# Turned values leave PSUM in one copy, and a piece of the sample's convolution is started during the prompt's output projection

## The chip, the cores and the metric

The kernel runs on one core of a Trainium2 chip. The metric is device time in microseconds (us) of one execution. The kernel before took 1496.22 us (median of three runs, 1496.03 to 1497.55); its profiled execution took 1495.0 us.

## The reference, cut to what matters

One layer of a bidirectional encoder trunk with shared weights is applied to two inputs: a prompt of 512 tokens and a sample of 1024 tokens, both 1024 wide, in float32.

```python
h = rmsnorm(x); z = h @ w_in                 # columns: q 512, k 128, v 128, ca 512, cb 512
a_out = window_attn(q, k, v, bias, band, sink)   # |q-k| <= 128, 8 heads, 2 key/value heads of 64
c = ca * sigmoid(cb)
c = dwconv(c, conv_dw_w, conv_dw_b)          # 31 taps along the sequence, 512 channels
c = silu(layernorm(c))
x = x + concat([a_out, c]) @ w_out
u = dwconv(rmsnorm(x) @ w_up, ffn_dw_w, ffn_dw_b)  # 3 taps, 2 x 2816 channels
x = x + (silu(u[:, :2816]) * u[:, 2816:]) @ w_down
y = rmsnorm(x)
```

## The kernel before

Every matrix product is made of three float32r products: each operand is split into a rounded high part (a ScalarE cast or activation) and a low part (operand minus high part, on VectorE or GpSimd), and TensorE adds hi x hi, hi x lo and lo x hi in one PSUM bank. Lines L315 to L317 are these three products of the input and up projections, L796 to L798 those of the output projection. Activations lie with channels on the 128 partitions and 512 tokens along the row.

PSUM has eight banks, each one tile of 128x512 float32: a (three), u (two), b (two) and c (one). Each kind of work may take certain letters. SBUF is cut into slots (h: 61 of 2 KB, q: 15 of 4 KB, and some others); a tile keeps its slot until its last reader has run. In the rows of a profile `h<-b` means that an h slot is written from a b bank.

The stages, with their rough times in the profile:

- **Input projection, 0 to 278 us.** `step` runs one chunk of 128 output columns for 512 tokens (24 matmuls), and `evac` takes the bank apart: convolution inputs go through a gate (L424 folds the sample's), keys and queries are split and stored, values are turned. For the values (`kind "v"`) the scaled tile is turned by four TensorE transposes (L456) into a fresh bank. Then for each of the two key/value heads, ScalarE casts its half of the columns (L463, 128x256), VectorE subtracts that from the bank to get the low part (L464), and for the sample the result is sent to DRAM (L466). This happens three times: once for the prompt, at 88 us, and twice for the sample, at 153 and 166 us. All four operations read the bank, and the sample's copies come back in `load_kv` after the projection. Beside the sample's chunks, `prompt_attention` runs as side work: scores L650, softmax L654, L663, turned scores L692 (cast L694, subtract L695), and the products with the values L706 and L707.
- **Prompt's output projection, 278 to 326 us.** The generator `prompt_out` loads the weights of w_out (L821 in pairs, L817 alone), splits them (`split_wo`: cast L828, subtract L829), runs `out_half` for four blocks of 128 tokens and two halves of the columns, and then `make_h2`, the second RMSNorm (scale L854) with its turn into eight tiles (`transposed`: L274, L276, L277; banks u, b and c). The loop `while out` counts its steps in n; past n = 18 every fourth step also starts one unit of the sample's attention.
- **Prompt's FFN, first half, 337 to 629 us,** with the rest of the sample's attention and its convolution ("late" work) beside it.
- **Sample's output projection, 630 to 720 us, then the sample's FFN and both down projections to the end.** TensorE's order from 720 us on is the same in both kernels.

The convolution runs in `taps`: a bank c accumulates most taps on VectorE (first tap L366, the others L352), a few taps per accumulator are made on ScalarE (L340, L343) and summed on GpSimd (L344), and L360 adds the two sums and frees the bank. `tick`, called with the matmul groups, raises `pace["credit"]`, and work is drawn from `mid` (the accumulator that is open), `convs` (the prompt's channels) or `late` (the sample's) while the credit is positive; a step costs 0.13 + 512/960 = 0.66 of it. The sample's first late set works on sums of neighbouring columns (`csum`) and has ten taps on VectorE.

The order of instructions on each engine comes from a scheduler that simulates the program written here and places what it finds ready first; the written order, the slots and the banks are its input. From then on each engine works strictly in its order.

## Time and profile before

| | us |
|---|---|
| median of three runs | 1496.22 |
| profiled execution, own time | 1495.0 |
| its span from first to last instruction | 1493.2 |
| TensorE busy | 1473.5 |
| VectorE busy | 1118.7 |
| ScalarE busy | 803.4 |
| GpSimd busy | 776.1 |

PE stands for TensorE, PEld for its weight loads, DVE for VectorE, ACT for ScalarE, POOL for GpSimd, SP for the engine whose queue issues most DMAs. A timeline row reads: start, duration, engine, line and operation, output from inputs, count, and in brackets the idle time of the engine before it with what ended that. Matmuls are pipelined, so one shows about 0.39 us though the next starts 0.23 us after it. A group row gives the count, the busy time and mean ns of one, and the idle time before its instructions.

### The profile page before, as it was taken

The page shows a single profiled execution, that of the slowest core. Times are in us where ns is not written, and L with a number is a line of the kernel's source. Part 1 is how long each engine was busy: PE and PEld are TensorE (multiplying, and loading weights), DVE is VectorE, ACT ScalarE, POOL GpSimd, SP SyncE. Part 2 cuts the span into 40 slices and gives each one's busy share as a digit, 9 for nine tenths or more (in the row PEclk, how much of TensorE's full clock was granted, in tenths as well). Part 3 has the DMA queues.
Part 4 walks back from the last instruction along what each step waited for, and adds up shares of the span by engine and source line. Part 5 has one row for each costly group of instructions (what it writes and reads, how often), then busy time and mean ns, then how long its engine had stood idle before and what let it go on. Part 6 is the DMA issues. An engine that isn't in the chain of part 4 may idle for free.

```text
span 1493.2 us, 19866 instructions
## 1 busy us (share of the span) xinstructions
PE 1473.5 (99%) x6736; PEld 1211.8 (81%) x6736; DVE 1118.7 (75%) x1512; ACT 803.4 (54%) x1421; POOL 776.1 (52%) x687
## 2 busy tenths in 40 slices
PE   9999999999999999999999999999999999999998
PEld 7788787878888888788788788888888888888886
DVE  6877945648988887675768888888887856577874
ACT  7524455567778776653465444454444543343355
POOL 3554353338779766332436565665555251135546
PEclk9999999999999999999999999999999999999999
DMA  9555331844444454663214333333332495356644
GB/s 369 193 153 146 95 104 35 240 162 140 123 141 135 131 179 142 215 208 106 71 57 141 134 128 126 128 124 123 129 133 79 144 330 173 117 194 216 221 166 162
DMA packets 124625, 228.19 MB, mean 153 GB/s; under 512 B 20419, under 2 KB 45763, under 8 KB 124396
## 3 DMA queue, kind: packets, MB, share of 16 engines
q1 hardware_dynamic: 124092, 226.37, 46.4%
q8 instruction: 53, 0.87, 0.2%
q10 hardware_dynamic: 432, 0.56, 0.1%
q14 instruction: 48, 0.39, 0.1%
HBM read 166.83 MB, written 61.10 MB: 153 GB/s over the span
## 4 chain that ended last, share of the span: by engine, by line
PE 87%; DVE 4%; DMA 3%; POOL 3%; ACT 2%; issue 2%; SPq 0%; POOLq 0%; DVEq 0%; ACTq 0%
PE w L1194 8%; PE w L1195 8%; PE w L1196 8%; PE w L1527 7%; PE w L1526 7%; PE w L1528 7%; PE b L315 4%; PE b L317 4%; PE b L316 4%; PE u L315 4%; PE u L317 4%; PE u L316 4%; PE a L650 1%; PE a L692 1%; PE u L797 1%
## 5 line engine op out<-in xcount | busy, mean ns | idle before, releaser
L163 POOL TENSOR_TENSOR q<-q,q 128x1024 fp32r<-128x1024 f32 x66 | 159.3, 2414 | 68.1 <-ACT q L162 43.4
L1074 POOL TENSOR_TENSOR q<-q,q 128x512 fp32r<-128x512 f32 x81 | 116.0, 1441 | 127.3 <-ACT q L1180 127.3
L1074 DVE TENSOR_TENSOR h<-h,h 128x512 fp32r<-128x512 f32 (+1 forms) x152 | 129.5, 881 | 57.8 <-ACT h L1082 23.1
L1528 PE MATMUL w<-h,h 128*128 128x512 f32 x432 | 168.1, 389 | 0.0
L1526 PE MATMUL w<-h,h 128*128 128x512 f32 x432 | 168.1, 389 | 0.0
L1527 PE MATMUL w<-h,h 128*128 128x512 f32 x412 | 160.3, 389 | 0.0
L1194 PE MATMUL w<-h,q 128*128 128x512 f32 x368 | 143.8, 391 | 1.1 <-ACT w L1285 0.7
L1196 PE MATMUL w<-h,q 128*128 128x512 f32 x368 | 143.7, 390 | 0.0
L1195 PE MATMUL w<-h,q 128*128 128x512 f32 x347 | 135.5, 390 | 0.0
L1082 ACT CAST h<-h 128x512 fp32r<-128x512 f32 x116 | 69.2, 620 | 105.4 <-DVE h L1074 30.8
L1074 POOL TENSOR_TENSOR h<-h,h 128x512 fp32r<-128x512 f32 (+1 forms) x38 | 52.2, 1375 | 141.7 <-ACT h L1509 110.4
L315 PE MATMUL b<-h,q 128*128 128x512 f32 x312 | 123.2, 395 | 1.9 <-DVE h L464 1.3
L317 PE MATMUL b<-h,q 128*128 128x512 f32 x312 | 122.4, 393 | 0.0
L316 PE MATMUL b<-h,q 128*128 128x512 f32 x312 | 122.1, 391 | 0.0
L315 PE MATMUL u<-h,q 128*128 128x512 f32 x272 | 106.8, 393 | 0.0
L316 PE MATMUL u<-h,q 128*128 128x512 f32 x272 | 106.8, 393 | 0.0
L317 PE MATMUL u<-h,q 128*128 128x512 f32 x272 | 106.7, 392 | 0.0
L162 ACT CAST q<-q 128x1024 fp32r<-128x1024 f32 x66 | 69.1, 1048 | 55.4 <-PE u L316 16.3
L352 DVE SCALAR_TENSOR_TENSOR c<-d,cvw,c 128x512 f32<-128x512 f32 x128 | 96.0, 750 | 1.6
L344 POOL TENSOR_TENSOR h<-h,h 128x512 f32<-128x512 f32 x62 | 81.7, 1318 | 27.1 <-ACT h L343 22.5
L1526 PEld LDWEIGHTS w<-h,h 128*128 128x128 f32 x432 | 81.1, 188 | 17.0
L1528 PEld LDWEIGHTS w<-h,h 128*128 128x128 f32 x432 | 81.1, 188 | 16.8
(476 smaller groups left out, 4002.5 us busy)
## 6 DMA issues: line engine op xcount, KB each, us to landing
q<-in_laid_w_up SPq DMA_DIRECT2D x88, 512.0 KB, 3.7
ga<-q SPq DMA_DIRECT2D x65, 256.0 KB, 2.2
h<-gap SPq DMA_DIRECT2D x57, 256.0 KB, 3.5
h<-ga SPq DMA_DIRECT2D x57, 256.0 KB, 3.5
h<-in_w_down SPq DMA_DIRECT2D x52, 256.0 KB, 3.4
q<-in_laid_w_in SPq DMA_DIRECT2D x22, 512.0 KB, 4.3
gap<-h SPq DMA_DIRECT2D x44, 256.0 KB, 3.1
q<-in_x_sample SPq DMA_DIRECT2D x15, 512.0 KB, 6.9
```

The lines of the kernel that those rows point to most:

```text
L163: (nc.vector if dve else nc.gpsimd).tensor_tensor(lo[:], raw[:], hi[:].bitcast(F32), op=ALU.subtract)
L315: nc.tensor.matmul(out, whi[:, kc, :], hi[:], start=(kc == 0), stop=False)
L316: nc.tensor.matmul(out, whi[:, kc, :], lo[:], start=False, stop=False)
L317: nc.tensor.matmul(out, wlo[:, kc, :], hi[:], start=False, stop=(kc == KC - 1))
L352: nc.vector.scalar_tensor_tensor(acc[:], src(t), w(t), acc[:], op0=ALU.mult, op1=ALU.add)
L1074: (eng or nc.vector).tensor_tensor(out, a, b, op=ALU.subtract)
L1194: nc.tensor.matmul(out, whi[:, s], hi[:], start=(start and c == 0), stop=False, **go)
L1195: nc.tensor.matmul(out, whi[:, s], lo[:], start=False, stop=False, **go)
L1196: nc.tensor.matmul(out, wlo[:, s], hi[:], start=False, stop=(stop and c == 3), **go)
L1526: nc.tensor.matmul(out, sh[:, c], th[:], start=(p == 0 and not seeded), stop=False, **go)
L1527: nc.tensor.matmul(out, sh[:, c], tl[:], start=False, stop=False, **go)
L1528: nc.tensor.matmul(out, sl[:, c], th[:], start=False, stop=(p == NPAIR - 1), **go)
```

## The change

Two edits. In the evacuation of the values, one ScalarE copy takes the whole turned bank into an SBUF tile; the casts read that tile, and the low parts are made on GpSimd instead of VectorE, also from that tile. The stores to DRAM follow both heads. In the loop around `prompt_out`, the steps n = 19 to 26 raise the credit by 0.3 each, once the prompt's channels are done, and draw late work from it: about four steps of the sample's first late accumulator. Lines behind the first edit are one higher in the profile after, lines behind the second five.

```diff
+OL = (18, 0.3, 26)
...
-            vs = []
-            for kv in range(NKV):
-                v = sb.tile([4, P], F32R)
-                head = slice(kv * HD, (kv + 1) * HD)
-                rest = slice((1 - kv) * HD, (2 - kv) * HD)
-                nc.scalar.copy(v[:, :, head], src[:, :, head])
-                nc.vector.tensor_tensor(v[:, :, rest], src[:, :, head], v[:, :, head].bitcast(F32), op=ALU.subtract)
-                if g == 1:
-                    nc.sync.dma_start(vsd[:, n, kv], v[:].bitcast(F32))
-                vs.append(v)
+            vs = [sb.tile([4, P], F32R) for _ in range(NKV)]
+            heads = [slice(kv * HD, (kv + 1) * HD) for kv in range(NKV)]
+            whole = sb.tile([4, P])
+            nc.scalar.copy(whole[:], src)
+            for v, head, rest in zip(vs, heads, heads[::-1]):
+                nc.scalar.copy(v[:, :, head], whole[:, :, head])
+                nc.gpsimd.tensor_tensor(v[:, :, rest], whole[:, :, head], v[:, :, head].bitcast(F32), op=ALU.subtract)
+            if g == 1:
+                for kv in range(NKV):
+                    nc.sync.dma_start(vsd[:, n, kv], vs[kv][:].bitcast(F32))
...
         advance(out)
         n += 1
+        if OL[0] < n <= OL[2] and (mid or not convs):
+            pace["credit"] += OL[1]
+            while late and pace["credit"] > 0:
+                pace["credit"] -= advance(mid[0] if mid else late)
```

Since the scheduler orders the whole program, the edits move instructions elsewhere too. Three places follow. In the rows the first number of a name is its slot or bank, the second the tile.

ScalarE at the sample's first values, before; `b0_49` is the bank with the turned values:

```order
L663 ACTIVATE h32_248_1523,s11_247_1519<-h32_248_1523,s10_246_1518 128x385
L463 CAST h44_243_1507<-b0_49_1502 128x4x64
L663 ACTIVATE h31_249_1529,s11_247_1519<-h31_249_1529,s10_246_1518 128x385
L663 ACTIVATE h15_250_1543,s11_247_1519<-h15_250_1543,s10_246_1518 128x385
L463 CAST h19_244_1511<-b0_49_1502 128x4x64
```

and after:

```order
L664 ACTIVATE h31_250_1527,s11_249_1523<-h31_250_1527,s10_248_1522 128x385
L462 COPY h16_246_1511<-b0_49_1504 128x512
L664 ACTIVATE h15_251_1533,s11_249_1523<-h15_251_1533,s10_248_1522 128x385
L464 CAST h44_244_1509<-h16_246_1511 128x4x64
L464 CAST h19_245_1510<-h16_246_1511 128x4x64
```

The copy L462 is the bank's only reader; both casts stand together behind the second softmax activation and read SBUF.

TensorE at the start of the prompt's output projection, before; `a1_122` is the last product of the prompt's scores and values, `u1_126` the first output bank:

```order
L706 MATMUL a1_122_2665<-h38_418_2646,h18_160_923 128x512
L315 MATMUL b0_123_2685<-h42_98_437,q8_400_2519 128x512
L316 MATMUL b0_123_2685<-h43_99_438,q8_400_2519 128x512
L317 MATMUL b0_123_2685<-h42_98_437,q10_401_2520 128x512
L707 MATMUL a1_122_2665<-q13_419_2647,h18_160_923 128x512
L706 MATMUL a1_122_2665<-q4_420_2661,h18_160_923 128x512
L707 MATMUL a1_122_2665<-q9_421_2662,h18_160_923 128x512
L796 MATMUL u1_126_2815<-h56_449_2783,h23_229_1421 128x512
```

and after:

```order
L771 MATMUL a2_118_2621<-ident_82,h38_415_2598 128x128 x4
L756 MATMUL u0_124_2714<-ident_82,h2_83_354 128x128
L756 MATMUL u0_124_2714<-ident_82,h27_141_744 128x128
L756 MATMUL u0_124_2714<-ident_82,h17_198_1177 128x128
L756 MATMUL u0_124_2714<-ident_82,h26_291_1808 128x128
L707 MATMUL a1_122_2671<-h38_421_2652,h18_160_921 128x512
L708 MATMUL a1_122_2671<-q13_422_2653,h18_160_921 128x512
L707 MATMUL a1_122_2671<-q4_423_2667,h18_160_921 128x512
L708 MATMUL a1_122_2671<-q9_424_2668,h18_160_921 128x512
L797 MATMUL u1_126_2821<-h56_452_2789,h23_230_1423 128x512
```

The projection's matmuls (L316 to L318, earlier L315 to L317) are all done ahead of this piece, the turn `a2_118` moved from among them (28 rows up) to here, and the four products and eight turns stand in a row. Slot h38 holds `h38_415`, which that turn reads, and then `h38_421`, the cast for the first product.

VectorE at the same place, after; `q13_422` is the subtract for the second product, L830 the weights' low parts:

```order
L417 TENSOR_TENSOR b0_123_2691<-b0_123_2691,d1_125_569 128x512
L761 BN_STATS s31_430_2719<-u0_124_2714 128x6
L830 TENSOR_TENSOR h42_465_2814<-h58_450_2785,h43_464_2813 128x512
L425 SCALAR_TENSOR_TENSOR c3_425_2686<-h29_416_2618,b0_123_2691 128x256x2
L762 BN_AGGR s32_431_2720<-s31_430_2719 128x2
L696 TENSOR_TENSOR q13_422_2653<-a0_120_2647,h38_421_2652 128x512
L830 TENSOR_TENSOR h55_453_2790<-q2_419_2636,h56_452_2789 128x512
L765 TENSOR_SCALAR h15_433_2726<-u0_124_2714,s32_431_2720,s0_432_2721 128x512
L830 TENSOR_TENSOR h53_455_2794<-q2_419_2636,h54_454_2793 128x512
L830 TENSOR_TENSOR h18_492_2986<-h9_480_2962,h21_491_2985 128x512
L830 TENSOR_TENSOR h58_496_3011<-h8_481_2964,h59_495_3010 128x512
```

Before, this engine's order had the splits of the first two weight pairs (`q2`, `q0`) ahead of the last evacuation; now they follow it, and the third chunk's low part comes nine operations behind `q13_422`.

TensorE at the end of the prompt's FFN, before; `u0_339` is the last up projection, `a2_332` the last scores:

```order
L317 MATMUL u0_339_6375<-h17_546_3298,q13_1028_6316 128x512
L650 MATMUL a0_333_6296<-q10_439_2763,h47_993_6070 128x256
L650 MATMUL a0_333_6296<-q8_440_2764,h47_993_6070 128x256
L796 MATMUL c0_346_6544<-h0_1051_6459,h51_1048_6453 128x512
L797 MATMUL c0_346_6544<-h56_1052_6460,h51_1048_6453 128x512
L798 MATMUL c0_346_6544<-h0_1051_6459,h10_1049_6454 128x512
L796 MATMUL c0_346_6544<-h46_1054_6465,h51_1048_6453 128x512
L692 MATMUL a1_336_6340<-ident_82,h49_996_6077 128x128
L692 MATMUL a1_336_6340<-ident_82,h52_997_6083 128x128
L692 MATMUL a1_336_6340<-ident_82,h30_998_6101 128x128
L692 MATMUL a1_336_6340<-ident_82,h32_999_6107 128x128
L650 MATMUL a2_332_6290<-q10_439_2763,h47_993_6070 128x256
```

and after:

```order
L693 MATMUL a1_336_6346<-ident_82,h13_999_6083 128x128
L693 MATMUL a1_336_6346<-ident_82,h12_1000_6089 128x128
L651 MATMUL a2_332_6296<-q10_442_2769,h16_996_6076 128x256
L651 MATMUL a2_332_6296<-q8_443_2770,h16_996_6076 128x256
L693 MATMUL a1_336_6346<-ident_82,h45_1001_6107 128x128
L693 MATMUL a1_336_6346<-ident_82,h1_1002_6113 128x128
L316 MATMUL u0_335_6331<-h32_545_3283,q11_1021_6253 128x512
L317 MATMUL u0_335_6331<-h14_546_3284,q11_1021_6253 128x512
```

The scores `a2_332` came after the last up projection; now they come among the matmuls of the last but one, 45 rows ahead of the last.

Two more moves have no rows here. On VectorE the ten `csum` taps of the late set, which stood behind the prompt's turn, now stand among the evacuations of the input projection, in rows 208 to 222 of its order, with only their ScalarE and GpSimd offloads left beside the output projection. Their bank c is not free again until after `make_h2`, whose turn therefore goes round the two b and two u banks.

## The prediction

> **What bounds the kernel now.** The first view is the head of the page: the span and the engines' shares.

> ```profile
> span 1493.2 us, 19866 instructions
> PE 1473.5 (99%) x6736; PEld 1211.8 (81%) x6736; DVE 1118.7 (75%) x1512; ACT 803.4 (54%) x1421; POOL 776.1 (52%) x687
> ```

> PE works in 1473.5 of 1493.2 us, so the change can take away only idle PE time, at most 19.7 us, and can add to it. PE's matmuls stay, so the time is a sum over places where PE waits. The second view, PE's list of waits, names them; the columns are total us, times, longest.

> ```profile
> PE a L706 <- ACT h L694: 1.8, 1, 1.8
> PE b L315 <- DVE h L464: 1.3, 1, 1.3
> PE c L274 <- DVE q L854: 0.5, 1, 0.5
> ```

> The third view gives each engine's load in stretches of 40 us where the change acts: after the length, busy us (and instructions) of PE, its weight loads, DVE, ACT and POOL, then PE's clock and the DMA's share.

> ```profile
> 120.00:160.00 40.00, 37.41 (x182) 30.84 (x181) 37.40 (x74) 19.81 (x46) 16.11 (x22) 1.00 0.43 132
> 200.00:240.00 40.00, 39.86 (x196) 33.27 (x195) 15.75 (x35) 19.50 (x40) 17.40 (x19) 1.00 0.36 99
> 280.00:320.00 40.00, 39.88 (x187) 32.74 (x186) 20.23 (x41) 16.63 (x39) 11.98 (x18) 1.00 0.79 234
> 600.00:640.00 40.00, 37.91 (x179) 30.48 (x178) 26.66 (x51) 26.64 (x54) 15.97 (x12) 0.96 0.76 255
> ```

> The two middle ones have next to no PE idle time to remove (39.86 and 39.88 of 40). The first lost 2.6 us at full clock, the last 2.1 us, and its clock is 0.96. The new order touches five places; I name them A to E in order of time and price each.

> **A, the sample's first turned values (152 to 157 us).** The timeline shows the chain on the bank.

> ```profile
> 153.62 0.35 ACT L463 CAST h<-b 128x256 fp32r<-128x256 f32 x1
> 154.52 0.62 PE L650 MATMUL a<-h,h 128*128 128x384 f32 x2 [1.08 <-DVE s L654]
> 156.03 0.37 ACT L463 CAST h<-b 128x256 fp32r<-128x256 f32 x1 [0.76 <-DVE h L464]
> 156.63 0.41 DVE L464 TENSOR_TENSOR h<-b,h 128x256 fp32r<-128x256 f32 x1
> 157.18 0.47 PE L315 MATMUL b<-h,q 128*128 128x512 f32 x1 [1.34 <-DVE h L464]
> ```

> Bank b is held from 153.62 until 157.04 because the second subtract stands behind other DVE work. PE idles 1.08 + 1.34 = 2.4 us there. After the change one ScalarE copy frees the bank. No 128x512 COPY is in this trace; the nearest rows are a 64x512 copy and a 128x512 cast.

> ```profile
> L714 ACT COPY h<-a 64x512 f32<-64x512 f32 x21 | 12.2, 582 | 12.7 <-PE a L707 12.5
> L694 ACT CAST h<-a 128x512 fp32r<-128x512 f32 x54 | 31.1, 577 | 12.1 <-PE a L692 8.3 <-DMA qsd<-h 3.2 <-DVE q L695 0.5
> ```

> I take 0.58. In the new order the copy stands behind one exponential, so it runs 153.6 to 154.2. PE takes the projection next, idle from 153.4 to about 154.2, 0.8 us: **A = -1.6** (bounds -2.4 to 0). The casts and the two GpSimd subtracts are hidden: the sample's values are read back only after the input projection. The nearest row for a subtract on POOL is twice as wide (1.32 us), so one costs between 0.66 and 1.32 and six cost 4 to 8 us of a POOL that is half idle; DVE loses 6 x 0.41 = 2.5 us. Were a ScalarE copy no faster than two casts and a wait, A would be 0.

> ```profile
> L344 POOL TENSOR_TENSOR h<-h,h 128x512 f32<-128x512 f32 x62 | 81.7, 1318 | 27.1 <-ACT h L343 22.5 <-DVE h L961 1.8 <-ACT h L340 1.8
> ```

> **B, 247 to 250 us.** Here PE waits for the low part of turned scores.

> ```profile
> 247.97 0.50 PE L707 MATMUL u<-q,h 128*128 128x512 f32 x1 [0.81 <-DVE q L695]
> ```

> The new order puts one L424 (1.10 us, next fence) ahead of that subtract; part of it falls into a wait that is there already: **B = +0.6** (0 to +1.1).

> **C, the start of the prompt's output projection.** The change's words put the convolution's taps beside this projection. The order doesn't: all ten of the channel's DVE taps go ahead into the input projection, to about 220 to 231 us, where DVE has 15.75 of 40 us busy. By the rows of L366 (place D) and L352, 0.81 + 9 x 0.75 = 7.6 us; they cost nothing there, and without that slack they would delay the projection's evacuations by up to as much.

> ```profile
> L352 DVE SCALAR_TENSOR_TENSOR c<-c,csum,c 128x512 f32<-128x512 f32 x36 | 27.0, 750 | 0.5
> L343 ACT ACTIVATE h<-c,csum 128x512 f32<-128x512 f32 x20 | 14.0, 720 | 1.7 <-DMA cvd<-h 1.6 <-PE u L798 0.2
> ```

> What does cost is that the loads of the first two weight pairs are issued later on SP, their splits move behind other DVE work, and the turned scores' last products move with them. Before, that start was nearly smooth:

> ```profile
> 282.57 0.39 PE L796 MATMUL u<-h,h 128*128 128x512 f32 x1
> 283.08 0.50 PE L797 MATMUL u<-h,h 128*128 128x512 f32 x1
> 283.42 0.40 PE L798 MATMUL u<-h,h 128*128 128x512 f32 x1
> 283.65 0.40 PE L796 MATMUL u<-h,h 128*128 128x512 f32 x1
> ```

> Matmuls follow each other at 0.23 us (283.42, 283.65); the step from 282.57 to 283.08 lost 0.28. Now the rows for the new order, from the timeline and from the groups of 230 to 330 us:

> ```profile
> 269.86 1.28 DVE L829 TENSOR_TENSOR h<-q,h 128x512 fp32r<-128x512 f32 x2
> ...
> 284.35 0.60 PE L770 MATMUL a<-ident,h 128*128 128x128 f32 x4
> 284.70 0.48 PE L796 MATMUL u<-h,h 128*128 128x512 f32 x1
> ```

> ```profile
> L829 DVE TENSOR_TENSOR h<-h,h 128x512 fp32r<-128x512 f32 x12 | 9.2, 782 | 4.7 <-ACT h L828 4.5
> L416 DVE TENSOR_TENSOR b<-b,d 128x512 f32<-128x512 f32 x2 | 1.4, 696 | 0.2 <-PE b L317 0.2
> L424 DVE SCALAR_TENSOR_TENSOR c<-q,b 128x512 f32<-128x512 f32 x2 | 2.2, 1102 | 0.0
> L760 DVE BATCH_NORM_STATS2 s<-u 128x6 f32<-128x512 f32 x2 | 1.4, 698 | 2.6 <-PE u L755 2.6
> L695 DVE TENSOR_TENSOR q<-a,h 128x512 fp32r<-128x512 f32 x3 | 2.0, 678 | 0.2 <-ACT h L694 0.2
> L776 ACT ACTIVATE q<-a,vecs 128x128 f32<-128x128 f32 x4 | 1.5, 456 | 0.5 <-PE a L770 0.5
> ```

> Call 0 the end of the input projection's last matmul. PE then turns eight tiles (0.35 for four, 284.35 to 284.70; so 0.7) and wants the first product of scores and values. Its operand is a ScalarE cast (0.58) that now stands behind four L776 (1.5), which need the first four turns: ready at about 0.4 + 1.5 + 0.6 = 2.5, a wait of 1.8. The second product needs the subtract that in DVE's order comes after an evacuation (0.70), a BN_STATS (0.70), a split (0.78) and an L424 (1.10): with its own 0.68 ready at 4.0, against PE at 2.7, a wait of 1.3. Eighteen matmuls and four turns later (4.0 + 4.5 = 8.5) PE needs the low part of the third weight chunk, nine DVE operations behind that subtract, most of them splits of 0.64 (two in 1.28) to 0.78. At 0.71 each it is ready at 4.0 + 6.4 = 10.4: a wait of 1.9. Sum 5.0, less the 0.28: **C = +4.7**. Bounds: +2, if the splits' order is harmless and only the first wait stays; +7, if the cast is also late behind splits that wait for their DMA.

> The clock belongs here too. At the end of the prompt's FFN the trace shows what idle time did to it.

> ```profile
> 628.92 0.48 PE L650 MATMUL a<-q,h 128*128 128x256 f32 x2
> 631.22 0.50 PE L706 MATMUL a<-h,h 128*128 128x512 f32 x1 [1.81 <-ACT h L694]
> 632.32 0.67 PE L797 MATMUL c<-h,h 128*128 128x512 f32 x1
> 632.79 0.63 PE L798 MATMUL c<-h,h 128*128 128x512 f32 x1
> ```

> After one wait of 1.81 us the step went from 0.23 to 0.47 us, and the stretch's mean clock fell to 0.96: 0.04 x 40 = 1.6 us lost. The waits at A, 2.4 us in two pieces, cost no clock (1.00 in 120 to 160 us). C has 1.8 + 1.3 us of waits close together, so I count one such drop: **clock at C = +1.6** (0 to +3.2).

> [...]

> **D, the prompt's second RMSNorm and turn (326 to 341 us).**

> ```profile
> 339.43 0.75 DVE L277 SCALAR_TENSOR_TENSOR h<-c,vecs,h 128x512 fp32r<-128x512 f32 x1 [0.40 <-ACT h L276]
> 340.69 0.81 DVE L366 TENSOR_SCALAR c<-c,csum,vecs 128x512 f32<-128x512 f32 x1
> ```

> The late convolution takes bank c at 340.69, after the turn has used it. With the new order the accumulator holds c through the turn, which has four banks instead of five. On POOL one more offloaded sum (L344, 1.32) stands ahead of the root (L146, L147) that releases L854, for which PE waits 0.5 already, and on ScalarE one more offload (L343, 0.72) ahead of the evacuations that free a bank for the first up projection. **D = +2.0** (1.3 + 0.7; bounds 0 to +3).

> **E, the end of the prompt's FFN (629 to 641 us).** The last scores were issued after the last up matmul (628.92), so nothing covered their softmax. The new order issues them 45 PE rows earlier, some 9 us of matmuls. The 1.81 us and the clock's 1.6 go, some 0.2 stays: **E = -3.2** (-3.6 to 0). The FFN between D and E keeps its work on PE, and DVE is lighter by the 7.6 us.

> **Sum:** -1.6 + 0.6 + 4.7 + 1.6 + 2.0 - 3.2 = +4.1. The profiled execution took 1495.0 us (its span and 1.8 around it), so 1499.1; the median, 1496.22, lies 1.2 above that execution, so 1500.3. I predict **1500**.

> **The rivals.** *Faster, 1492.* A and E hold, and the start of the output projection stays as smooth as it was: DVE is busy only 20.23 of 40 us there and catches up. Then 1496.2 - 1.6 - 3.2 + 0.6 = 1492. For it: the two gains remove waits that the list names, with a simple mechanism. Against it: the order of DVE is fixed, and idle time elsewhere in the stretch can't be used.
> *No measurable change, 1496.* C costs 2 without a clock drop, D 2: -1.6 + 0.6 + 2 + 2.0 - 3.2 = -0.2. For it: the terms have both signs. The change then does little of what it says, since the taps moved to a place where DVE idled.
> *The clock holds at C, 1498.7.* All else as in my sum: 4.1 - 1.6 = +2.5. The trace shows 2.4 us of split waits at A that left the clock alone.
> *Slower still, 1504.* ScalarE's cast at C waits behind a split whose weight lands late: C = +7 and two drops of the clock, +3.2. That is 2.3 + 1.6 = 3.9 above the sum. It decides once a weight that SP loads behind the prompt's residual rows lands after the eight turns.

> **How the numbers follow.** My forecast has a chance of 0.35, the held clock 0.15, slower still 0.1, no change 0.18, faster 0.22. About 0.2% (3 us) is what a measurement of this kernel tells from no change, so faster means under 1493.2 and slower over 1499.2. The forecast and the slower rival give slower, and a third of the held-clock case, 0.5 in all; the faster rival, 0.22; the rest, 0.28. The range, **1492.5 to 1505**, reaches to the rivals on both sides; the likeliest case's own is 1497 to 1503.

> **What would show it.** In the changed profile: no wait of L316 for the value split and under 1 us of PE idle at 152 to 157 us (A); waits of L707, L708 and L798 for L695, L696 and L830 at about 277 to 290 us with 3 to 7 us together, and a clock under 1.00 there (C); the first up matmul 2 us or more later against the last output matmul (D); clock 1.00 in 600 to 640 us and no 1.8 us wait (E). The prediction is wrong if PE's idle time at C stays under 1 us, or if new waits appear inside the FFN.

## The result, and the profile after

The changed kernel took 1504.23 us (median of five, 1501.05 to 1506.96) against 1497.24 us (1496.03 to 1498.29) for the kernel before: a ratio of 1.0051, 95% interval 1.0040 to 1.0063, so about 7.6 us slower. Its profiled execution took 1502.96 us, its span 8.0 us longer than before.

The head of the page of the changed kernel:

```profile
span 1501.2 us, 19884 instructions
PE 1475.2 (98%) x6736; PEld 1216.5 (81%) x6736; DVE 1118.2 (74%) x1506; ACT 803.7 (54%) x1424; POOL 770.6 (51%) x693
```

PE has the same 6736 instructions; it idles longer. Its list of waits (total us, times, longest) shows where:

```profile
PE a L707 <- ACT h L695: 3.2, 1, 3.2
PE b L275 <- DVE q L855: 2.8, 1, 2.8
PE u L651 <- DVE q L717: 1.9, 1, 1.9
...
PE u L797 <- DVE q L802: 1.4, 1, 1.4
PE a L651 <- DVE h L717: 1.3, 1, 1.3
PE a L708 <- DVE q L696: 1.3, 1, 1.3
PE u L708 <- DVE q L696: 1.0, 1, 1.0
PE c L798 <- DVE h L830: 1.0, 1, 1.0
PE b L316 <- ACT h L462: 0.9, 1, 0.9
```

In order of time: the value bank now costs 0.9 us (before 1.08 + 1.34); at 244 to 252 us there are three waits of 0.5, 1.0 and 1.9 us; at 277 to 283 us 3.2 + 1.3; at 297 us 1.4; at 338 to 344 us 1.3 + 2.8; at 645 to 652 us 1.0, 0.6 and 0.2. In these stretches (length, then busy us and instructions of PE, its loads, DVE, ACT, POOL, then PE's clock) the clock fell as well:

```profile
276.00:300.00 24.00, 18.11 (x74) 14.05 (x73) 18.81 (x26) 14.04 (x30) 9.49 (x9) 0.86 0.88 284
326.00:350.00 24.00, 19.86 (x101) 16.78 (x100) 14.01 (x28) 17.55 (x36) 15.14 (x23) 0.86 0.31 110
640.00:656.00 16.00, 14.20 (x67) 10.38 (x66) 13.25 (x21) 10.31 (x20) 6.82 (x7) 1.00 0.94 317
```

The start of the output projection, in the timeline, ScalarE first, then PE:

```profile
267.58 0.49 ACT L670 ACTIVATE d<-d,s 128x256 f32<-128x256 f32 x1
273.86 0.62 ACT L829 CAST h<-h 128x512 fp32r<-128x512 f32 x1 [5.79 <-DMA h<-in_laid_w_out]
...
277.22 1.65 ACT L829 CAST h<-h 128x512 fp32r<-128x512 f32 x3
278.77 1.50 ACT L777 ACTIVATE q<-a,vecs 128x128 f32<-128x128 f32 x4
280.15 0.58 ACT L695 CAST h<-a 128x512 fp32r<-128x512 f32 x1
```

```profile
280.79 0.79 PE L707 MATMUL a<-h,h 128*128 128x512 f32 x1 [3.20 <-ACT h L695]
282.85 0.79 PE L708 MATMUL a<-q,h 128*128 128x512 f32 x1 [1.27 <-DVE q L696]
```

ScalarE stood still for 5.79 us because the next row in its order is a weight split whose DMA had not landed. Twelve more operations stand between that split and the cast (280.15) for which PE waits 3.2 us. This is one queue, in order, with a late DMA at its head.

The prompt's second turn, GpSimd, then VectorE and PE:

```profile
335.59 2.40 POOL L164 TENSOR_TENSOR q<-q,q 128x1024 fp32r<-128x1024 f32 x1 [1.99 <-DVE q L802]
337.95 2.63 POOL L345 TENSOR_TENSOR h<-h,h 128x512 f32<-128x512 f32 x2
...
340.79 0.19 POOL L147 TENSOR_SCALAR rs<-s 128x1 f32<-128x1 f32 x1
341.07 0.55 POOL L148 TENSOR_TENSOR rs<-rs,nhalf 128x1 f32<-128x1 f32 x1
341.59 1.25 POOL L719 TENSOR_TENSOR h<-h,h 64x512 fp32r<-64x512 f32 x1
```

```profile
341.65 1.74 DVE L855 TENSOR_SCALAR q<-q,rs 128x1024 f32<-128x1024 f32 x1 [1.98 <-POOL rs L148]
343.45 0.69 PE L275 MATMUL b<-ident,q 128*128 128x128 f32 x2 [2.81 <-DVE q L855]
```

The last root (L147, L148) stands behind an up-weight split and two offloaded sums; the scaling that PE waits for follows it.

### The profile page after: what moved, and what is told of

Same layout as the page of the kernel before. It is cut to its first block, busy times and chain, and to the rows that moved or that the text cites. A ratio compares the mean times of both kernels' runs of the same rounds, so it can differ in the third digit from the quotient of the medians.

```text
span 1501.2 us, 19884 instructions
## 1 busy us (share of the span) xinstructions
PE 1475.2 (98%) x6736; PEld 1216.5 (81%) x6736; DVE 1118.2 (74%) x1506; ACT 803.7 (54%) x1424; POOL 770.6 (51%) x693
## 4 chain that ended last, share of the span: by engine, by line
PE 87%; DVE 4%; DMA 4%; POOL 2%; ACT 2%; issue 2%; SPq 0%; POOLq 0%; DVEq 0%; ACTq 0%
PE w L1199 8%; PE w L1200 8%; PE w L1201 8%; PE w L1531 7%; PE w L1532 7%; PE w L1533 7%; PE b L316 4%; PE b L318 4%; PE b L317 4%; PE u L318 4%; PE u L316 4%; PE u L317 4%; PE a L651 1%; PE a L693 1%; DMA h<-in_laid_w_out 1%
## 5 line engine op out<-in xcount | busy, mean ns | idle before, releaser
L316 PE MATMUL b<-h,q 128*128 128x512 f32 x328 | 129.0, 395 | 1.8 <-ACT h L462 0.9
L317 PE MATMUL b<-h,q 128*128 128x512 f32 x328 | 128.6, 393 | 0.0
L318 PE MATMUL b<-h,q 128*128 128x512 f32 x328 | 128.2, 392 | 0.0
L316 PE MATMUL u<-h,q 128*128 128x512 f32 x256 | 100.6, 393 | 0.0
L318 PE MATMUL u<-h,q 128*128 128x512 f32 x256 | 100.5, 393 | 0.0
L317 PE MATMUL u<-h,q 128*128 128x512 f32 x256 | 100.2, 391 | 0.0
L353 DVE SCALAR_TENSOR_TENSOR c<-d,cvw,c 128x512 f32<-128x512 f32 x128 | 96.0, 750 | 1.6
```

The source lines that it names most:

```text
L316: nc.tensor.matmul(out, whi[:, kc, :], hi[:], start=(kc == 0), stop=False)
L317: nc.tensor.matmul(out, whi[:, kc, :], lo[:], start=False, stop=False)
L318: nc.tensor.matmul(out, wlo[:, kc, :], hi[:], start=False, stop=(kc == KC - 1))
L353: nc.vector.scalar_tensor_tensor(acc[:], src(t), w(t), acc[:], op0=ALU.mult, op1=ALU.add)
```

## Experiments: which part of the change costs

The orders of the two edits separate cleanly: the values' evacuation alone moves PE's rows 653 to 812, the draw of late work alone rows 974 to 3324 (up to 733 us in the profile before). Both were run alone. Runs e1 to e4 were timed against 1495.70 us for the kernel before, e5 to e8 in another session against 1496.28 us, so differences between runs are given by the ratios.

**The values' evacuation alone (e1).** The loop's window is made empty:

```diff
-OL = (18, 0.3, 26)
+OL = (18, 0.3, 18)
```

> The values' evacuation of the change alone; the loop around the prompt's output projection as before. Theory 1 (the new copy frees the bank early, the draw of late work is what costs): PE's idle time at 152 to 157 us falls from 2.4 to about 0.9 us and nothing else changes, so 2 us faster, ratio 0.9985 to 0.9990. Rival (the subtracts on GpSimd or the extra ScalarE pass cost the time): slower by 3 us or more, ratio over 1.002.

Measured: 1491.83 us against 1495.70, ratio 0.9977 (0.9966 to 0.9987), 3.5 us faster. Its list of waits has the bank's wait at 0.9, as in the changed kernel; the other waits are those of the kernel before, a little shorter or longer:

```profile
PE a L707 <- ACT h L695: 1.5, 1, 1.5
...
PE b L316 <- ACT h L462: 0.9, 1, 0.9
PE c L275 <- DVE q L855: 0.8, 1, 0.8
```

Theory 1 holds in its sign. The gain is larger than the 1.5 us of idle time. In the two profiled executions, 4.0 us apart, PE's matching rows (the same row's start in each) give 2.1 us at the bank, 0.9 at the end of the FFN (its wait is 1.5 us instead of 1.8, and no half clock follows) and 1.1 at the two waits at 745 and 824 us. So about half of it lies outside the edited place; a possible reason stands with e8.

**The draw of late work alone (e2).** The kernel before with the five lines in the loop.

> The draw of late work in the loop alone; the values' evacuation as before. Theory 1: the waits at 245 to 252 us, at 278 to 283 us and at 338 to 344 us stay as in the changed kernel, so 8 to 10 us slower than before, ratio 1.0055 to 1.0070. Rival (the values' edit costs): within 0.2% of before.

Measured: 1509.68 us, ratio 1.0102 (1.0086 to 1.0117), 15 us slower, well over the 8 to 10 expected. The same waits stand at the same places:

```profile
PE a L707 <- ACT h L695: 3.9, 1, 3.9
PE c L798 <- DVE h L830: 2.3, 1, 2.3
PE b L275 <- DVE q L855: 2.2, 1, 2.2
PE u L797 <- DVE q L802: 2.1, 1, 2.1
PE u L651 <- DVE q L717: 1.9, 1, 1.9
```

So the loss is the draw's. The two edits don't add up exactly: -3.5 and +15 us make +11.5, and together they cost 7.6. In the profiles e2 ends 6.7 us behind the changed kernel, and 3.6 of them stand at the value bank, where e2 keeps the two waits and half clock follows them (156.8 us), which in the profile before cost no clock. Another half-clock stretch (255.8 us), which the changed kernel doesn't have, makes most of the next 2.2 us.

**The drawn taps held back (e3).** The whole change, with the first tap's weight made from a column of the output projection's first result (times zero), so that the ten taps can't be placed before it:

```diff
+            lead = sm(1)
+            nc.vector.tensor_scalar(lead[:], pin.pop()[:, 0:1], 0.0, csum[:, c:c + 1], op0=ALU.mult, op1=ALU.add)
...
+        if n == OL[0] + 1:
+            pin.append(xr[0])
```

Its PE order equals that of e1 up to row 1244 and that of the changed kernel from row 1409 on.

> The whole change, but the weight of the first tap of the drawn accumulator is made by a one-column operation that reads the residual rows of the first output block (times zero), so its ten taps can't stand ahead of the output projection. Theory 1a (the taps that moved into the input projection displace the attention chain and the weight loads in the scheduler's order): the waits at 245 to 252 us and at 278 to 283 us and the halved clock behind them go, those at 338 to 344 us stay, so 1493 to 1498 us. Rival 1b (drawing the work during the output projection costs, wherever its taps stand): 1502 us or more, with a wait of over 2 us at the start of the output projection.

Measured: 1490.97 us, ratio 0.9968 (0.9956 to 0.9980): by the ratios some 12 us below the changed kernel, and lower than the 1493 to 1498 expected. VectorE now runs the taps (L367, L353) between the weight splits (L838) and residual sums (L810) of the output projection, where the change's words put them, and PE goes through its start with one wait of 0.47 us:

```profile
288.36 0.81 DVE L367 TENSOR_SCALAR c<-c,s,vecs 128x512 f32<-128x512 f32 x1
289.13 0.69 DVE L838 TENSOR_TENSOR h<-h,h 128x512 fp32r<-128x512 f32 x1
289.74 0.75 DVE L353 SCALAR_TENSOR_TENSOR c<-c,csum,c 128x512 f32<-128x512 f32 x1
290.40 0.68 DVE L810 TENSOR_TENSOR q<-u,q 128x512 f32<-128x512 f32 x1
```

```profile
270.00:300.00 30.00, 29.53 (x136) 24.19 (x135) 25.55 (x38) 14.75 (x28) 11.82 (x13) 1.00 0.85 258
326.00:345.00 19.00, 15.98 (x78) 12.93 (x77) 17.01 (x31) 17.29 (x36) 12.36 (x13) 0.91 0.39 130
625.00:650.00 25.00, 22.74 (x107) 18.41 (x106) 18.09 (x29) 15.37 (x29) 9.37 (x9) 0.93 0.73 246
```

Theory 1a holds: the place of the ten taps decides. The draw itself, with its taps beside the output projection, neither costs nor gains measurably: the interval overlaps that of e1 (0.9966 to 0.9987), so the gain here is the values' edit. The waits at the second turn are smaller (1.1 + 1.2 us) but there, with a clock of 0.91; and at 633 us a wait of 2.3 us for a weight split (L838) has taken the place of the one for the cast.

**Only a free bank c (e4).** The kernel before with one letter less:

```diff
-    use.update(attn="a", norm="b", turn="ubc")
+    use.update(attn="a", norm="b", turn="ub")
```

> The kernel before, with one letter taken away: the prompt's second turn uses banks u and b, not c. No work is drawn in the loop and the values are evacuated as before. Theory 1a says that a free bank c is what lets the late taps move ahead into the input projection: the waits at 245 to 252 us and 278 to 283 us appear here too, 1501 us or more. Rival 1b (the draw itself is the cause): no wait over 1 us there, within 0.3% of before.

Measured: 1510.81 us, ratio 1.0101 (1.0087 to 1.0115). No work is drawn here, yet PE's order equals that of e2 for its first 1222 rows, with the taps at the same place in the input projection. The first tap, in the changed kernel and here:

```profile
217.50 0.81 DVE L367 TENSOR_SCALAR c<-c,csum,vecs 128x512 f32<-128x512 f32 x1
```

```profile
222.30 0.80 DVE L366 TENSOR_SCALAR c<-c,csum,vecs 128x512 f32<-128x512 f32 x1
```

The waits at the start of the output projection are alike (3.7, 1.3 and 2.7 us, in e2 3.9, 0.8 and 2.1):

```profile
PE a L706 <- ACT h L694: 5.0, 3, 3.7
PE u L797 <- DVE h L829: 3.2, 2, 2.7
PE u L650 <- DVE q L716: 1.9, 1, 1.9
```

Of the 16.3 us by which this profile is longer than that of before, 15.1 are lost by 300 us, ahead of the turn; that the turn has four banks instead of five costs little beside that. So the mechanism is the bank as a fence. In the kernel before, the turn's use of c stood ahead of the late taps in the program and held them back. The draw puts the taps ahead of the turn in the program (e4 lets the turn leave c alone), and in both cases the scheduler finds c free while the input projection still runs and hoists them there. Why the hoist makes it issue the weight loads later and reorder the splits, I have not traced.

**The sums ahead of the root (e5).** As e3, with the first drawn accumulator's offloads summed on VectorE:

```diff
-                nc.gpsimd.tensor_tensor(pacc[:], pacc[:], pr[:], op=ALU.add)
+                (adder or nc.gpsimd).tensor_tensor(pacc[:], pacc[:], pr[:], op=ALU.add)
```

> As the pinned kernel (e3), but the offloaded taps of the first drawn accumulator are summed on VectorE, so GpSimd has two 1.3 us sums fewer ahead of the last root of the prompt's second norm. Theory (GpSimd's queue is what makes the scaled rows late at 328 to 331 us): PE's waits there, 1.1 + 1.2 us in e3, fall to under 1 us and the clock stays whole there: 1 to 3 us faster than e3, 1488 to 1490 us. Rival (the turn's four banks instead of five are what waits): the waits stay within 0.5 us of e3's and the time within 1 us of 1491.

Measured: 1494.21 us, ratio 0.9987 (0.9979 to 0.9996), 3 us slower than e3: a miss. The waits at the turn did halve (0.5 + 0.6 us), and the clock stayed whole there. But two others stand right behind:

```profile
334.87 0.50 PE L716 MATMUL a<-h,h 128*128 128x512 f32 x1 [0.54 <-DVE h L704]
336.76 0.47 PE L316 MATMUL b<-h,q 128*128 128x512 f32 x1 [1.04 <-DVE h L278]
```

These four and one of 0.2 us come to 2.8 us from 326 to 337 us, against 3.0 from 328 to 339 us in e3. GpSimd's queue set the first wait; without it the evacuation (L278) that frees the bank for the first up projection ends last. The theory was right about the waits and wrong about the time; the rival's time was off too. The loss lies at the end of the FFN, whose order changed as well: there the profile of e5 goes from 1.1 us ahead of e3 to 2.5 behind (waits of 1.3, 0.5 and 0.8 us at 630 to 634 us, and half clock for 6.8 us).

**The split at 633 us on GpSimd (e6).** As e3, with one more of four weight splits on GpSimd:

```diff
-WOP, WOA, DW, DW2 = 1, 5, 2, 3
+WOP, WOA, DW, DW2 = 1, 5, 2, 2
```

> As the pinned kernel (e3), but of four splits of the sample's output weights two instead of three are made on VectorE. Theory (PE's 2.26 us wait at 633 us is for a weight split that stands on VectorE behind the FFN's convolution): that wait and the half clock after it go, 2 to 4 us faster than e3, 1487 to 1489 us. Rival (the weight lands late, or GpSimd's slower subtract takes its place): a wait of 1.5 us or more stays at 625 to 645 us, 1490 us or more.

Measured: 1495.51 us, ratio 0.9993 (0.9985 to 1.0002), 3.7 us slower than e3. The wait of 2.3 us and its half clock went, as the theory said, but five waits of 0.5 to 1.1 us between 633 and 642 us (3.8 together) took their place, and a new one of 1.7 us appeared at 745 us. The rival holds for the time, though no single wait of 1.5 us is left at that place: the time at the end of the FFN isn't that one split.

**The low parts back on VectorE (e7).** As e1, with one word changed:

```diff
-                nc.gpsimd.tensor_tensor(v[:, :, rest], whole[:, :, head], v[:, :, head].bitcast(F32), op=ALU.subtract)
+                nc.vector.tensor_tensor(v[:, :, rest], whole[:, :, head], v[:, :, head].bitcast(F32), op=ALU.subtract)
```

> The values' evacuation alone, as e1, but with the low parts on VectorE as in the kernel before (from the copied tile). Theory (the early freeing of the bank is the whole gain): the same as e1, ratio 0.9967 to 0.9990. Rival (the gain is VectorE's lighter load): back to before, ratio over 0.999.

Measured: 1491.20 us, ratio 0.9971 (0.9960 to 0.9983), the same as e1. The gain is the copy, not the engine of the subtracts.

**TensorE's clock (e8).** The kernel before, with 2 to 6 extra copies of a bank onto another, of the same data, at nine places in the sample's FFN where TensorE waits for that copy; TensorE's order is row for row that of before.

```diff
-            nc.scalar.copy(s["x"][:, R], s["wy"][:, R])
+            for _ in range(1 + {3: 2, 5: 3, 7: 4, 9: 5, 11: 6, 13: 3, 15: 4, 17: 2, 19: 5}.get(j, 0)):
+                nc.scalar.copy(s["x"][:, R], s["wy"][:, R])
```

Measured: 1523.64 us, ratio 1.0184 (1.0169 to 1.0200). In every trace here that has more than one half-clock record, these begin whole multiples of 3.413 us apart, to within 0.02 us, so I cut e8's span into these stretches. Each pair is a stretch with a stall and the one behind it; the column before the last two is the clock.

```profile
826.36:829.77 3.41, 1.42 (x6) 1.21 (x7) 2.18 (x2) 2.41 (x5) 2.39 (x2) 1.00 0.69 231
829.77:833.18 3.41, 3.41 (x9) 2.65 (x9) 0.86 (x2) 0.43 (x1) 0.00 (x0) 0.50 0.00 0
867.32:870.73 3.41, 1.69 (x8) 1.08 (x7) 1.97 (x2) 3.35 (x7) 2.50 (x2) 1.00 0.71 228
870.73:874.15 3.42, 3.42 (x16) 2.81 (x17) 1.51 (x3) 0.76 (x2) 0.00 (x0) 1.00 0.02 7
908.28:911.69 3.41, 1.21 (x6) 0.67 (x4) 1.93 (x3) 3.35 (x8) 2.50 (x2) 1.00 0.75 231
911.69:915.11 3.42, 2.90 (x7) 2.32 (x8) 1.21 (x2) 0.47 (x1) 0.00 (x0) 0.50 0.00 0
```

With PE busy 1.42 or 1.21 us of 3.41 the next stretch is at half clock (the full one at 829.77 carries 9 matmuls, the one at 870.73 16); with 1.69 it is at full clock. The stall at 909.49 us lasted 2.72 us, less than a stretch. Half clock follows four of the nine places, those with 1.99 us or more of idle time in one stretch; the other five have 1.72 at most. Theory 2 holds at these nine places, and the rival is out. But "half a stretch" is no sharp limit. Among the shorter matmuls of the attention less sufficed in the same run: 1.36 us of idle in one stretch at 331 us and 1.59 us at 154 us were followed by half clock. And in the profile before, 1.91 us of idle time in the stretch from 1485.82 us, where PE's last matmul ends, were not. Why is open.

The stretches bear on e1. The 2.4 us of waits at the value bank fell into two stretches in the profile of before and cost no clock there; in the profiles of e2, e4 and e8, with the same two waits, half clock follows them at 156 to 157 us. So the waits cost 2.4 us in some executions and about 1.6 more in others, and the copy leaves 0.9 us of the waits and none of the half clock. That this explains the rest of the 3.5 us is argued, not shown; in the profiled pair, where before kept its clock there, the rest lay at the later waits and in the half clock behind one of them.

## Why the prediction was right, and where its terms were off

The forecast, slower and 1500 us, had the sign and most of the mechanism. The measured median lies at the upper end of the range, outside the likeliest case's own 1497 to 1503, and beside the rival of 1504 us, which had a chance of 0.1; +7.6 us against +4 means that the terms behind the sign were too small. In the profiled execution:

- **A, -1.6.** PE's idle time fell from 2.42 to 0.91 us, -1.5. A full-bank copy took 0.57 us (0.58 assumed); a subtract on GpSimd 0.74 us, near the low end of 0.66 to 1.32.
- **B, +0.6.** The waits at 244 to 247 us are 0.48 + 1.03 us against 1.04: +0.5. I missed a wait of 1.91 us at 249.5 us, where scores wait for the bank of a product (L717).
- **C, +4.7, and clock +1.6.** The first two waits were 3.2 and 1.3 us against 1.8 and 1.3 predicted. The first was longer for nearly the cause I had put into the rival of 1504 us, ScalarE's cast behind a split whose weight lands late; the weight came before the eight turns (split at 273.86 us), not after them, but the queue had already lost 5.8 us. The third, 1.9 us, did not come: PE was at half clock from 280.4 us on and arrived later. Instead the first output row waits 1.4 us at 297 us for residual rows, of which SP issues the last load only at 291.97 us. The clock was half not for one stretch but for two (280.4 to 287.2 us), of which, less the 1.7 us that were idle, half is lost: 2.6 us.
- **D, +2.0.** PE idled 4.4 us (waits of 1.3 + 2.8 + 0.3) against 1.5 before: +2.9. The queue that I named, GpSimd's with one sum more ahead of the root, is in the rows; the clock that it took with it, again two stretches (341.8 to 348.7 us) or up to 2.6 us, was not in my sum. I counted a clock drop at C alone.
- **E, -3.2.** The clock stayed whole (that 1.6 us was busy time at half clock, so the gain was not bounded by PE's idle time alone, as I had written), and the 1.8 us wait for the cast went, but three others came to 1.8 us: -0.7 and -1.6. In e3 one of them is 2.3 us, with half clock. "Some 0.2 stays" was wrong: at this place whatever ends first uncovers the next.
- Outside the five places, two waits later in the sample's FFN (1.25 us at 745 us, 0.74 at 824 us) shrank to 0 and 0.34 us, which I had not looked for.

These sum to +10.7 us with all clock terms (the 0.28 us that C lost before taken off), where the span grew by 8.0. PE's matching rows in the two profiles show where the 2.7 between come from: -0.2 us ahead of A, -2.1 at A, +2.5 at B, +8.1 at C, +4.1 at D, -2.4 at E and -2.1 at the two later waits. So D is overstated by 1.4: most of what PE ran in its two half-clock stretches are short turns and scores (17 in the second, full one), and half clock cost about 1.2 us there instead of 2.6. A and the two later waits gained 0.5 or so more than their idle time.

That the median stayed inside the range is in part luck: the 2.1 us gained at the two later waits stood nowhere in the prediction, and without them, going by the profile, it would have come out at about 1506.

The step that failed most in the prediction is the clock: by the rows it cost about 2.6 us at C and 1.2 at D, where I had 1.6 and nothing; the wait of 1.9 us that I missed at B comes next. I had one drop in the trace, priced it rightly at 1.6 us, and then counted drops by a feel for "close together", where counting the idle time by stretches (2.46 us in one of them at D) shows that D loses its clock as well. The rival "no change" had C at 2 us without a clock drop, and no such thing came; the "faster" rival lives in e1 and e3, that is, without the hoisted taps.

The cause behind C was put in the right place (taps hoisted, weight loads and splits behind other work) but not followed to its root. I priced the hoist at nothing, as VectorE had room at 220 to 231 us. It had, and yet e3 and e4 show that the hoist is what makes B and C: not through VectorE's time (in the changed profile it is busy 12.4 of the 22 us from 230 to 252 us, between the taps and the end of B's waits) but through the scheduler's order, in which everything behind those taps moves.

## What to carry to other kernels

A tile that is shared by two pieces of work can also be a fence between them in a scheduled program. Who frees a bank earlier, or takes it earlier in the program, should look at which later work is now ready early, and pin that work where it is meant to run: a one-column operation that reads a late result (0.2 us here) turned a loss of 7.6 us into a gain of about 5, of which the values' copy alone makes 3.5. A copy that empties a PSUM bank at once was worth its extra pass (0.57 us) here, where TensorE waited for that bank. And idle time on TensorE should be counted per stretch of 3.41 us: in the FFN of e8, 1.99 us or more of it in one stretch was followed by a clock of 0.50 in the next, by estimate half of 3.41 us or about 1.7 us on top, and 1.72 us or less was not (in its attention 1.36 us was).

## What the runs showed of the hardware

TensorE's clock stayed at half for a second stretch where the half-clock stretch itself still had 1.6 to 1.7 us of waits (280.4 and 341.8 us in the changed kernel), though as much idle time at full clock (1.71 us at 249.7 us) did not halve it. Less was enough elsewhere, 0.64 us in the half-clock stretch at 633.5 us of e5, while 0.63 us at 347.9 us of e2 was not; what decides is open. The grid of stretches starts at a different place in each of the ten traces, so the same waits can fall into one stretch or into two. That this is why the changed kernel scatters by 6 us over five runs and e1, whose longest wait is 1.5 us, by 1.7 over eight is argued only; e4, with waits up to 3.7 us, scatters by 1.5 over four.

The scaling L855 took 1.74 us at 341.65 us, where GpSimd ran L719 (341.59 to 342.84 us), against 0.75 to 0.77 us in its other three rows in the changed kernel and in all four of the kernel before (L854, 747 to 755 ns). What made that one longer was not shown; no run here tested it.
